# Block products for the third group of the down projection in layer 0's second feed-forward block

## Chip, cores, metric

One core of a Trainium2 chip runs the whole kernel in one launch. The metric is the device time of that launch in microseconds (us), the median of several runs. Engines are named as in the profile: PE (TensorE, matmuls), PEld (its weight loads), DVE (VectorE), ACT (ScalarE), POOL (GpSimd), SP (SyncE, here a queue that only issues transfers).

## The reference, cut to what matters

Two layers over 528 tokens (512 and 16 meta tokens) of width 1024. Each layer is feed-forward, mixer, feed-forward; the last layer is followed by a norm. All in float32.

```
def swiglu(x, w_gate, w_up, w_down):            # D_FF = 2816
    return (jax.nn.silu(x @ w_gate) * (x @ w_up)) @ w_down

for l in range(DEPTH):                          # DEPTH = 2
    h = h + 0.5 * swiglu(rmsnorm(h, norm_gains[l, 0]), ffn_w_gate[l, 0], ffn_w_up[l, 0], ffn_w_down[l, 0])
    h = h + mixer(rmsnorm(h, norm_gains[l, 1]), ...)
    h = h + 0.5 * swiglu(rmsnorm(h, norm_gains[l, 2]), ffn_w_gate[l, 1], ffn_w_up[l, 1], ffn_w_down[l, 1])
return rmsnorm(h, final_norm)[:, N_META:]
```

The case concerns `ffn_w_down[0, 1]`, the down projection of the second feed-forward block of layer 0, which the kernel calls block (0, 1).

## The kernel before, in words

**Layout.** h is held transposed on the chip, as 8 tiles of 128 channels by 528 tokens (`hall`, `h(m)`). Every float32 operand of a matmul is split into a rounded part and a residual: `whi` (L310, ACT) and `wlo` (L311, DVE) for weights, `hi` and `lo` for the moving operand. A product takes three matmuls for each pair of tiles: hi by hi, hi by lo, lo by hi. Half of the tokens, 264, go into one matmul.

**Block products.** Gate and up projections use Strassen's method in Winograd's form: a 2 x 2 split of both matrices, seven block products (numbered 1 to 7) in place of eight. For the weights the blocks 11, 12 and 22 are loaded as they are (`DIRECT`), the four others are sums, made by accumulating transfers on POOL's queue (L224), by ACT negations (L219, L277), and in part by DVE. For the moving operand, `Norm.pair(j)` makes from two tiles of h seven parts, each split into hi and lo (lines 526 to 552: ACT L532, L539, L544, DVE L540, L545, L547, L548, L550, L551).

**Groups.** The 22 hidden tiles come as 11 pairs, in groups of 4, 4 and 3 pairs (`GROUPS`). After the pairs of a group, the group's share of the down projection is added to h. It can go two ways:

- direct: `down(g, m, first, last)` runs `product` (L488) for each output tile m over the group's hidden tiles. In the third group, two of the tiles have begun between the products of the group's last pair, tiles 0 to 3 are held until the last two hidden tiles are there, tiles 4 to 7 follow one by one. When tile m is complete, `add_to_h` adds it (L587), `lower_h` scales h(m) by the norm factor (L592), and `done(m)` starts the next block's operand.
- by block products: `operands_of`, `operand` and `difference` (L700, L701, L703, L706, L710) make the moving operands from the hidden tiles, and `fast_down(g, dq, c, part)` (matmuls L745) runs product c for quad dq (four tiles of h each). Each result is added at once to two tiles of h by DVE (L753). In the third group the last eleven products come in the order `CLOSING`, and `PACE = 0` has all eight `lower_h` and `done` stand behind the last of them in program order.

**Which way.** `fast_groups(f)` gives the number of groups that go by block products: all three for the blocks in `ALL_FAST`, two for the others. With `f = (l, f)`:

```
GROUPS = (4, 4, 3)
ALL_FAST = [(0, 0), (1, 0)]
CLOSING = tuple(zip((1, 0, 1, 0, 0, 0, 1, 1, 1, 1, 1), "16273456734"))
def fast_groups(f):
    return len(GROUPS) - (f not in ALL_FAST)
```

`ffn_steps` lists the steps of a block: P is a gate/up product, D a direct piece of the down projection, O the making of operands, S a block product of the down projection. `weight_plan` turns them into the order in which weights are loaded. A direct third group takes its weights from `wts` in 6 slabs of 512 KB; a block-product group loads 5 blocks a quad from `win` (384 KB each in the third group) and adds 4 accumulating transfers a quad.

**What comes after a block.** Blocks (0, 0) and (1, 0) are followed by the mixer; their `done` is `b.chunk`, one plain operand a tile (L516, L517) and its square. Block (0, 1) is followed by block (1, 0); its `done` is `d.pair_of`, which runs `Norm.pair` once both tiles of a pair are there. Block (1, 0) begins with products 1 and 2 of pairs 0 and 1, then 6 and 5 of pair 0; at the latter the squares of h are summed (L526) and the mean of the norm is a matmul against a constant (L494).

**Order.** The program is written in one order and a planner, run when the kernel is built, moves instructions ahead on each engine by readiness and program order; on the chip each engine then runs its own list in order. Weights are made up to three products ahead (`AHEAD_MADE`) into four buffers each for `whi` and `wlo`, and fetched up to nine loads ahead into three buffers.

Of the kernel before, what the change touches and what calls it, by code (L numbers as in the profile page):

```python
# [39 lines left out]


GROUPS = (4, 4, 3)
ALL_FAST = [(0, 0), (1, 0)]
LAST = [sum(GROUPS[: g + 1]) - 1 for g in range(len(GROUPS))]
QUADS = 2
LATE = 5
# [9 lines left out]
def fast_groups(f):  # L56
    return len(GROUPS) - (f not in ALL_FAST)

# [1375 lines left out]
```

## Time and profile before

| | |
|---|---|
| time, median of 3 runs | 2187.26 us (2186.92 to 2187.61) |
| span of the profiled execution | 2185.6 us |
| the profiled execution's own time | not given apart; the median is 1.7 us above the span |
| PE busy | 2149.1 us, 98% |
| DVE busy | 1802.6 us, 82% |
| ACT busy | 1245.9 us, 57% |
| third group of block (0, 1), direct | 1026.9 to 1111.7 us |
| third group of block (0, 0), block products | 279.6 to 362.5 us |
| third group of block (1, 0), block products | 1374.2 to 1456.9 us |

The span runs from the first to the last instruction. Busy time is the union of an engine's instructions; a matmul's record overlaps the next one's, so the pace of matmuls is read from their starts. Row forms: a timeline row gives start, length, engine, line, operation, output and inputs, shape, count and, in brackets, the idle time before it and what ended it; a group row gives count, busy time and mean; a wait row gives total, times and longest.

### The profile page before, as it was taken

How to read it: one execution, taken by the hardware profiler on the slowest of the kernel's cores; microseconds unless marked ns; L12 is line 12 of the kernel's file. 1: busy time of each engine (PE TensorE's matmuls, PEld its weight loads, DVE VectorE, ACT ScalarE, POOL GpSimd, SP SyncE). 2: the span in 40 equal slices, each digit the busy share in tenths (PEclk: the TensorE clock that was granted, in tenths of full speed). 3: DMA queues.
4: the chain of work that ended last, by engine and by line, in shares of the span. 5: the costliest groups of instructions: out<-in, count | busy, mean ns of one | idle time of the engine just before them, and what ended most of it. 6: DMA issues, size and time to landing. Idle time of an engine off the chain costs nothing.

```text
span 2185.6 us, 40161 instructions
## 1 busy us (share of the span) xinstructions
PE 2149.1 (98%) x16434; PEld 2056.1 (94%) x16434; DVE 1802.6 (82%) x2751; ACT 1245.9 (57%) x1844; POOL 119.0 (5%) x140
## 2 busy tenths in 40 slices
PE   7999999999999999999999999999999999999998
PEld 7999999989999999999999999988788888999997
DVE  8887979776976689888789979797779767997986
ACT  8545556444784556454575455574557836554544
POOL 1100000000000000010010000000000001000100
PEclk9999999999999999999999999999999999999999
DMA  9866755212113467676567667553121146775751
GB/s 286 218 195 182 202 154 139 82 51 76 49 40 123 130 177 180 202 185 183 167 162 187 199 181 204 153 140 97 49 78 49 49 135 152 199 204 178 196 162 68
DMA packets 91223, 320.32 MB, mean 147 GB/s; under 512 B 10144, under 2 KB 12576, under 8 KB 91040
## 3 DMA queue, kind: packets, MB, share of 16 engines
q1 hardware_dynamic: 70048, 246.58, 33.9%
q0 software_dynamic: 19584, 69.21, 17.6%
q8 instruction: 129, 2.11, 0.4%
q10 hardware_dynamic: 1408, 1.97, 0.3%
q14 instruction: 54, 0.44, 0.1%
HBM read 294.65 MB, written 2.10 MB: 136 GB/s over the span
## 4 chain that ended last, share of the span: by engine, by line
PE 83%; DVE 9%; ACT 4%; DMA 2%; issue 2%; SPq 0%; DVEq 0%; ACTq 0%
PE ss L621 36%; PE mm L488 15%; PE ss L745 14%; PE ss L488 7%; DVE wlo L311 3%; PE sm L488 2%; DMA w<-win 2%; PE sm L1125 1%; PE ss L1100 1%; ACT whi L310 1%; PE ss L494 1%; DVE h L753 1%; PE sm L1141 1%; PE ss L1101 1%; PE sm L1142 1%
## 5 line engine op out<-in xcount | busy, mean ns | idle before, releaser
L621 PE MATMUL ss<-xc,whi 128*128 128x264 f32 (+1 forms) x4928 | 903.1, 285 | 11.3 <-ACT whi L310 7.4
L621 PEld LDWEIGHTS ss<-xc,whi 128*128 128x128 f32 x4928 | 764.5, 189 | 14.9 <-ACT whi L310 8.0
L621 PE MATMUL ss<-xc,wlo 128*128 128x264 f32 (+1 forms) x2464 | 700.6, 285 | 4.0 <-DVE wlo L311 4.0
L311 DVE TENSOR_TENSOR wlo<-w,whi 128x1024 fp32r<-128x1024 f32 (+2 forms) x355 | 423.7, 1200 | 66.7 <-ACT whi L310 66.3
L621 PEld LDWEIGHTS ss<-xc,wlo 128*128 128x128 f32 x2464 | 465.0, 189 | 5.9 <-DVE wlo L311 5.9
L310 ACT CAST whi<-w 128x1024 fp32r<-128x1024 f32 (+2 forms) x355 | 362.1, 1036 | 169.3 <-PE ss L621 80.1
L488 PE MATMUL mm<-x,whi 128*128 128x264 f32 (+1 forms) x1712 | 385.5, 315 | 0.0
L488 PEld LDWEIGHTS mm<-x,whi 128*128 128x128 f32 x1712 | 278.1, 188 | 16.3 <-issue 1.0
L745 PE MATMUL ss<-g,whi 128*128 128x264 f32 (+1 forms) x1520 | 284.3, 285 | 3.6 <-DVE h L753 1.7
L488 PE MATMUL mm<-x,wlo 128*128 128x264 f32 (+1 forms) x856 | 266.3, 316 | 0.0
L745 PEld LDWEIGHTS ss<-g,whi 128*128 128x128 f32 x1520 | 236.2, 188 | 7.5 <-DVE g L706 3.6
L745 PE MATMUL ss<-g,wlo 128*128 128x264 f32 (+1 forms) x760 | 215.2, 283 | 0.0
L625 ACT COPY c<-ss 128x528 f32<-128x528 f32 (+1 forms) x132 | 78.4, 594 | 239.0 <-PE ss L621 238.7
L310 ACT CAST whi<-raw 128x1024 fp32r<-128x1024 f32 x114 | 119.3, 1048 | 130.7 <-PE mm L488 94.2
L311 DVE TENSOR_TENSOR wlo<-raw,whi 128x1024 fp32r<-128x1024 f32 x114 | 139.0, 1220 | 57.2 <-ACT whi L310 53.2
L488 PEld LDWEIGHTS mm<-x,wlo 128*128 128x128 f32 x856 | 159.6, 188 | 8.5 <-issue 0.5
L745 PEld LDWEIGHTS ss<-g,wlo 128*128 128x128 f32 x760 | 143.0, 188 | 0.0
L224 POOL DMA_DIRECT2D w<-win x64 | 56.1, 876 | 1453.2 <-DVE t L1261 342.0
L745 PE MATMUL ss<-c,whi 128*128 128x264 f32 (+1 forms) x608 | 115.5, 285 | 0.3
L311 DVE TENSOR_TENSOR wlo<-s,whi 128x1024 fp32r<-128x1024 f32 (+1 forms) x94 | 112.2, 1195 | 1.6 <-ACT whi L310 1.4
L467 ACT ACTIVATE c<-c 128x528 f32<-128x528 f32 (+1 forms) x88 | 56.5, 642 | 98.5 <-DVE c L671 98.4
L488 PE MATMUL ss<-g,whi 128*128 128x264 f32 (+2 forms) x516 | 103.6, 310 | 0.0
(270 smaller groups left out, 3379.1 us busy)
## 6 DMA issues: line engine op xcount, KB each, us to landing
w<-win SPq DMA_DIRECT2D x333, 512.0 KB, 4.4
raw<-wts SPq DMA_DIRECT2D x114, 512.0 KB, 3.3
w<-win POOLq DMA_DIRECT2D x60, 512.0 KB, 7.5
s<-win POOLq DMA_DIRECT2D x26, 512.0 KB, 7.5
w<-s POOLq DMA_DIRECT2D x26, 512.0 KB, 6.1
w<-win SPq DMA_DIRECT2D x20, 384.0 KB, 3.6
s<-w POOLq DMA_DIRECT2D x8, 512.0 KB, 7.4
h<-xt SPq DMA_DIRECT2D x3, 528.0 KB, 6.0
```

Source lines behind the costliest of these rows:

```text
L224: self.nc.gpsimd.dma_start(t, src, accum_op=ALU.add)
L310: nc.scalar.copy(hi[:, cs], w[:, cs])
L311: nc.vector.tensor_tensor(lo[:, cs], w[:, cs], hi[:, cs].bitcast(F32), ALU.subtract)
L467: prev_act[0] = S.activation(*args, **kw).ins
L488: TE.matmul(acc.half[i][:width], lhs, rhs[:, acc.spans[i]], start=first, stop=last)
L494: TE.matmul(a, weights, x[:, hs], start=True, stop=True)
L621: TE.matmul(acc[:, j], a[:, j, k], b[:, at], start=bool(begin and k == 0 and i == 0), stop=k == len(x) - 1 and i == 2, skip_group_check=no ...
L625: W.behind = S.copy(part(st, q), acc).ins
L745: closing[0] = TE.matmul(acc[:, j], a[:, j, k], xs[b][:, k], start=bool(begin and k == 0 and i == 0), stop=k == n - 1 and i == 2, skip_gro ...
L753: V.tensor_tensor(to, to, acc, ALU.add)
L1100: TE.matmul(s[:n, i, :HF], lhs, kh[:, hs], start=True, stop=False)
L1101: TE.matmul(s[:n, i, :HF], lhs, kl[:, hs], start=False, stop=True)
```

## The change

Block (0, 1) is added to `ALL_FAST`, so that its third group also goes by the seven block products, in the steps that blocks (0, 0) and (1, 0) already take. Nothing else in the source changes; `ffn_steps`, `weight_plan` and the layout of the weights in memory follow from it.

```
 GROUPS = (4, 4, 3)
-ALL_FAST = [(0, 0), (1, 0)]
+ALL_FAST = [(0, 0), (0, 1), (1, 0)]
 LAST = [sum(GROUPS[: g + 1]) - 1 for g in range(len(GROUPS))]
```

## The prediction, on record before the result

> **What bounds the kernel now.** I read the page first (span, busy times), then the stage windows, then the waits of TensorE, then the groups of VectorE instructions in two windows.
>
> ```profile
> span 2185.6 us, 40161 instructions
> PE 2149.1 (98%) x16434; PEld 2056.1 (94%) x16434; DVE 1802.6 (82%) x2751; ACT 1245.9 (57%) x1844; POOL 119.0 (5%) x140
> ```
>
> TensorE is busy 98% of the span, so a matmul removed counts in full only if VectorE (82%) keeps pace. The question is whether it does so at this place. Three windows show the third group of three feed-forward blocks, from the start of its last unbroken run of gate/up products to the first matmul of what follows. The first is the block that changes; the other two already close with block products (layer 0 first block, layer 1 first block). Columns: length, then busy time and count of PE, PEld, DVE, ACT, POOL, granted clock, DMA share, GB/s.
>
> ```profile
> 1026.93:1111.67 84.74, 84.74 (x697) 84.74 (x696) 67.25 (x97) 48.15 (x66) 6.12 (x7) 1.00 0.60 161
> 279.55:362.62 83.07, 81.75 (x663) 80.77 (x662) 72.33 (x99) 49.77 (x67) 7.88 (x9) 1.00 0.56 149
> 1374.21:1456.93 82.72, 81.45 (x661) 80.64 (x660) 72.31 (x99) 49.61 (x67) 7.87 (x9) 1.00 0.56 150
> ...
> 1430.00:1457.75 27.75, 26.48 (x207) 25.55 (x207) 27.48 (x38) 18.50 (x25) 1.76 (x2) 1.00 0.58 151
> ```
>
> In the block to be changed TensorE never rests (84.74 of 84.74). In its twins it rests 1.3 us, and in the last 27.75 us VectorE is busy 27.48: it is full there, not TensorE. The waits of TensorE in the twin's stage are two, both on VectorE:
>
> ```profile
> PE ss L745 <- DVE h L753: 0.8, 2, 0.6
> PE ss L745 <- DVE g L706: 0.4, 1, 0.4
> ```
>
> **The change, part by part.** The direct product is 8 output tiles x 6 slices x 3 terms x 2 halves = 288 matmuls. The block products are 2 quads x 7 products x 3 slices x 2 x 3 terms = 252. So 36 go, which is also 697 less 661. At 84.74/697 = 0.122 us each that is 4.4 us at most.
>
> Term 1, the stage. The edited block should look like its twin in layer 1: same shapes, same steps, same blocks ahead of it. Whole stage against whole stage: 82.72 - 84.74 = **-2.0 us** (the layer 0 twin gives 83.07, that is -1.7). Of the 4.4 us, 1.3 go to the two waits and the rest to the slightly longer pace of the block products.
>
> What this term holds without a price of its own: the seven operands' subtractions and residuals (L706, L710, L701), 14 additions to h (L753) for 8 (L587), 14 weight casts and residuals of 768 columns for 6 of 1024, six fewer hidden-tile splits. They are all in the twin's VectorE 72.3 us against 67.3. ScalarE goes from 48.2 to 49.6 us and has room; its work lies beside TensorE's.
>
> Transfers: 6 loads of 512 KB leave the SP queue and 10 of 384 KB come; 8 accumulating transfers come to POOL's queue. I cost them at nothing: in the twin's stage the DMA share is 0.56 against 0.60, and no TensorE wait there is on a transfer. The next block's first loads and sums move behind them on SP and POOL. What could hurt is the buffer of the next first weight block, free only after the last group's negated block is taken:
>
> ```profile
> 1436.95 0.84 ACT L277 ACTIVATE s<-w 128x768 f32<-128x768 f32 x1 [0.40 <-DVE wlo L311]
> 1087.47 0.88 POOL L224 DMA_DIRECT2D s<-win  x1 [25.26 <-ACT s L219]
> ```
>
> In the twin that is 1456.93 - 1436.95 = 20 us before the stage ends; before, the next block's first accumulation starts 24 us before. The summed blocks are wanted only after four products (4 x 24 x 0.122 = 11.7 us) more, so some 30 us remain for a few transfers. If that cover is gone, TensorE waits at the fifth product.
>
> Term 2, the hand-over. This is where the block differs from its twins: they are followed by the mixer, this one by the next feed-forward block, whose operands are built in pairs of seven block sums, not in plain chunks. Before, the direct product finishes h tile by tile, 4.4 us apart, and VectorE lowers h (L592) and builds pairs 0 to 3 meanwhile. With the block products, the first quad's tiles are final only after the sixth of eleven closing turns and the rest with the last two, and the code emits all eight L592 and the four pairs behind the last turn; the planner moves forward only what fits between the additions to h. So work that lay beside matmuls comes at the end. Its price is the work VectorE still owes when the matmuls end. First what it did before from 1090 to the matmul of the norm's mean (L494), the point where TensorE waits for it:
>
> ```profile
> 1090.00:1132.76 42.76, 41.51 (x337) 41.04 (x337) 40.60 (x70) 31.07 (x50) 5.25 (x6) 1.00 0.63 151
> L540 DVE TENSOR_TENSOR xc<-t,xc 128x264 fp32r<-128x264 f32 (+1 forms) x16 | 8.8, 561 | 0.6 <-ACT xc L539 0.5
> L311 DVE TENSOR_TENSOR wlo<-w,whi 128x1024 fp32r<-128x1024 f32 x7 | 8.5, 1216 | 0.8 <-ACT whi L310 0.8
> L592 DVE SCALAR_TENSOR_TENSOR h<-h,rs 128x528 f32<-128x528 f32 x8 | 5.6, 700 | 0.1
> L587 DVE TENSOR_TENSOR h<-h,ss 128x528 f32<-128x528 f32 x8 | 5.5, 693 | 0.0
> L526 DVE TENSOR_TENSOR t<-t,t 128x528 f32<-128x528 f32 x7 | 4.9, 704 | 0.4
> L550 DVE TENSOR_TENSOR t<-t,t 128x264 f32<-128x264 f32 x4 | 1.7, 424 | 0.0
> ...
> L551 DVE TENSOR_TENSOR t<-t,t 128x264 f32<-128x264 f32 x4 | 1.7, 422 | 0.0
> L631 DVE TENSOR_TENSOR c<-c,ss 128x528 f32<-128x528 f32 x2 | 1.4, 694 | 0.0
> L311 DVE TENSOR_TENSOR wlo<-raw,whi 128x1024 fp32r<-128x1024 f32 x1 | 1.2, 1224 | 1.0 <-ACT whi L310 1.0
> L311 DVE TENSOR_TENSOR wlo<-s,whi 128x1024 fp32r<-128x1024 f32 x1 | 1.2, 1217 | 0.0
> ```
>
> (L550, L548, L547, L545, L551 are five such groups of 1.7.) The groups add up to 45.6 us, the engine is busy 40.6: neighbours overlap, so a sum of rows counts 0.89. It is full to 40.6/42.76 = 95%. Now how much of the following block's share the twin had done when its last addition to h ended, at 1457.75:
>
> ```profile
> L753 DVE TENSOR_TENSOR h<-h,ss 128x528 f32<-128x528 f32 x14 | 9.5, 698 | 0.3 <-PE ss L745 0.2
> L311 DVE TENSOR_TENSOR wlo<-raw,whi 128x1024 fp32r<-128x1024 f32 x2 | 2.4, 1220 | 0.0
> L592 DVE SCALAR_TENSOR_TENSOR h<-h,rs 128x528 f32<-128x528 f32 x3 | 2.0, 699 | 0.0
> L517 DVE SCALAR_TENSOR_TENSOR x<-h,par,x 128x528 fp32r<-128x528 f32 x2 | 1.5, 760 | 0.0
> ```
>
> Two weight residuals, and 2.0 + 1.5 = 3.5 us of lowering and operands. The full engine leaves no more. So still owed up to L494: L592 5.6, pairs 8.8 + 5 x 1.7 = 17.3, squares L526 4.9, L631 1.4, six of the eight residuals of the next block 6 x 1.22 = 7.3; together 36.5, less 3.5 = 33.0; times 0.89 = 29.4 us if VectorE never rests, 30.9 us if it rests as before. TensorE's side before:
>
> ```profile
> 1111.67 0.41 PE L621 MATMUL ss<-xc,whi 128*128 128x264 f32 x2
> 1132.76 1.13 PE L494 MATMUL ss<-t,const 128*128 128x264 f32 x4 [1.05 <-DVE t L526]
> 1135.85 0.51 PE L621 MATMUL ss<-xc,whi 128*128 128x264 f32 x2 [0.74 <-ACT c L625]
> ```
>
> From the next block's first matmul to L494: 21.1 us. After: 1457.75 - 1456.93 = 0.8, plus 29.4 to 30.9, so 30.2 to 31.7; the hand-over grows by 9.1 to 10.6 us. If two of the six residuals (for the products behind L494) come after the squares, 2 x 1.22 x 0.89 = 2.2 less, 6.9. The likely order lies between; I take **+9.0 us**. TensorE's cover is gone in pieces: of a new pair's share TensorE has 4 products x 6 x 0.122 = 2.9 us to do, VectorE (17.3 + 5.6)/4 x 0.89 = 5.1 us.
>
> Sum: -2.0 + 9.0 = **+7.0 us** on the execution's span of 2185.6, that is 2192.6. The median of the runs, 2187.26, is 1.7 us above the span; I keep that and forecast 2194.3.
>
> **One rule weighed.** TensorE ran slower at the start of the execution, though the granted clock reads 1.00 there:
>
> ```profile
> 15.06 0.64 PE L621 MATMUL ss<-xc,whi 128*128 128x264 f32 x2
> ...
> 15.72 0.64 PE L621 MATMUL ss<-xc,whi 128*128 128x264 f32 x2
> 19.14 0.41 PE L621 MATMUL ss<-xc,whi 128*128 128x264 f32 x2
> 0.00:10.00 10.00, 2.02 (x6) 1.44 (x6) 5.12 (x13) 7.32 (x13) 1.08 (x5) 1.00 0.83 293
> 10.00:20.00 10.00, 7.94 (x33) 6.54 (x32) 9.12 (x21) 9.35 (x17) 1.69 (x3) 1.00 1.04 346
> 1133.85 0.41 PE L621 MATMUL ss<-xc,whi 128*128 128x264 f32 x2
> ```
>
> The same pair of matmuls took 0.64 us at 15.7 and 0.41 at 19.1. Short waits later did not bring that back (0.41 again 1.1 us after the 1.05 us wait at L494). The Trainium skill, "TensorE: Matmul & The Clock Gate", section "Why this matters for your kernels", says that no idle gaps above about 3 us should stand between bursts, since an idle window brings the half clock back. By that rule the sum would be rival 3's, since the new waits are bursts of 2.9 us in every 5.1 us, or of 1.5 us where only two products have their weights.
>
> **The rivals.**
> 1. Not slower: VectorE reaches the pairs during the closing turns, and the hand-over costs nothing. Then only term 1 is left: 2187.26 - 2.0 = 2185.3. It decides from the point where VectorE does 9 us more of the next block's work before the last block product ends. For it: the first quad's tiles are final some 10 us before the end. Against: the 27.48 of 27.75 us above.
> 2. The hand-over is set by the pairs alone, not by the squares behind them: TensorE gets more products ahead of L494 and the waits of 1.05 + 0.74 us vanish. Pairs are done 0.8 + (5.6 + 17.3 - 3.5) x 0.89 = 18.1 us after the last block product; TensorE has 11.7 us of products, if it can run them as operands come: 6.4 us lost. -2.0 + 6.4 - 1.8 = +2.6, 2189.9. For it: operands are awaited part by part, as the start shows below (TensorE begins at 7.36 with a pair whose last part is written at 9.34). Against: TensorE's order is fixed, and before it stood still at L494 with other products in hand.
> 3. The slow rate returns at the hand-over: up to the 39 matmuls of the start's two windows at 0.22 us (from 15.06 to 15.72 three matmuls in 0.66 us) for 0.122, about +4 on top: 2198.3. Against: the single gaps would be 2 to 3.5 us, at the edge.
>
> ```profile
> 7.36 0.81 PE L621 MATMUL ss<-xc,whi 128*128 128x264 f32 x2 [7.36 <-ACT whi L310]
> 9.34 0.71 DVE L540 TENSOR_TENSOR xc<-t,xc 128x528 fp32r<-128x528 f32 x1
> ```
>
> **How the numbers follow.** Forecast 0.56 (2194.3), rival 2 0.22, rival 3 0.14, rival 1 0.08. The range leaves out rival 1 and the upper part of rival 3: 2188 to 2198.5; the forecast's own, from 6.9 to 10.6 us of hand-over, is 2192.2 to 2195.9. A change within 0.2% (4.4 us) is about what a measurement of this kernel cannot tell from none: rival 2 and most of rival 1 fall there, the forecast and rival 3 are slower. Faster needs the whole 4.4 us and no wait: 0.04.
>
> **What would show it.** Right: 36 matmuls fewer; third group of 82.7 us; then TensorE waits on L540, L592 or L311 between about 1108 and 1135, VectorE above 95% there, L494 some 30 us after the last L745 of that group. Wrong: L592 and pairs already in the closing turns, or waits on transfers of the next block's weights, or matmul pairs of 0.64 us.

## The result, and the profile after

The changed kernel takes 2204.52 us (median of 5 runs, 2203.55 to 2207.06) against 2187.26 us for the kernel before (2186.36 to 2188.10): the ratio is 1.0078, with a 95% interval of 1.0066 to 1.0090. It is 17.3 us slower, where the prediction said 7.0 us slower with a range up to 2198.5. The page of the changed kernel shows that the matmuls went and the time did not:

```profile
span 2201.5 us, 40177 instructions
PE 2151.9 (98%) x16398; PEld 2056.2 (93%) x16398; DVE 1819.3 (83%) x2779; ACT 1256.8 (57%) x1861; POOL 125.9 (6%) x148
```

TensorE has 16398 matmuls for 16434, the 36 fewer that were counted, and yet it is busy 2.8 us longer (2151.9 for 2149.1). Fewer matmuls in more busy time means that some ran slower. The windows say where. The first row is the third group up to the first matmul of the next block, the second goes from there to L494, the others are stretches inside (columns as in the windows above: behind the five engines come the granted clock, the DMA share and GB/s):

```profile
1027.09:1120.48 93.39, 84.63 (x661) 83.17 (x660) 75.62 (x108) 52.97 (x71) 11.24 (x13) 0.96 0.64 163
1120.48:1148.35 27.87, 23.22 (x156) 21.36 (x157) 26.80 (x47) 21.92 (x37) 3.60 (x5) 0.88 0.70 161
1105.90:1112.20 6.30, 0.02 (x2) 0.01 (x1) 1.02 (x3) 0.89 (x2) 0.86 (x1) 0.92 1.08 211
1112.20:1117.94 5.74, 5.74 (x25) 5.51 (x25) 4.72 (x6) 3.63 (x5) 0.00 (x0) 0.50 0.82 249
1128.50:1134.70 6.20, 4.26 (x16) 3.36 (x15) 6.20 (x14) 4.37 (x10) 0.00 (x0) 0.50 0.50 98
```

The stage starts at 1027.09, 0.2 us from where it started before, so nothing ahead of it matters. It is 93.39 us long instead of 84.74: **+8.65 us**, where -2.0 was forecast. The hand-over up to L494 is 27.87 us instead of 21.09: **+6.8**. From L494 to the restart of the products 4.71 us go by instead of 3.09: **+1.6**. That is 17.05 us, of 17.3 between the medians (the two profiled spans lie 15.9 apart; the rest is made up later in the run). Inside the stage, 6.30 us hold no matmul to speak of (0.02 us busy), and the 5.74 us behind them are full of matmuls at a granted clock of 0.50.

The waits of TensorE over this stretch, and the rows at which the stages end:

```profile
PE ss L745 <- ACT whi L310: 6.3, 1, 6.3
PE ss L621 <- ACT xc L539: 3.1, 2, 1.7
PE ss L621 <- ACT c L625: 2.1, 1, 2.1
PE ss L745 <- DVE h L753: 1.1, 2, 0.9
PE ss L621 <- DVE h L753: 0.9, 1, 0.9
...
PE ss L494 <- DVE t L526: 0.5, 1, 0.5
```

```profile
1112.20 1.32 PE L745 MATMUL ss<-g,whi 128*128 128x264 f32 x3 [6.28 <-ACT whi L310]
1120.48 0.48 PE L621 MATMUL ss<-xc,whi 128*128 128x264 f32 x2 [0.89 <-DVE h L753]
1126.26 0.70 PE L621 MATMUL ss<-xc,whi 128*128 128x264 f32 x2 [1.42 <-ACT xc L539]
1130.61 0.90 PE L621 MATMUL ss<-xc,whi 128*128 128x264 f32 x2 [1.65 <-ACT xc L539]
1148.35 1.13 PE L494 MATMUL ss<-t,const 128*128 128x264 f32 x4 [0.51 <-DVE t L526]
1153.06 0.51 PE L621 MATMUL ss<-xc,whi 128*128 128x264 f32 x2 [2.11 <-ACT c L625]
```

The largest wait by far, 6.28 us, is one that the twin does not have: a block product of the closing stage waits for its weights' rounded part. The chain of work names what stood behind that:

```profile
1097.01 3.16 DMA w<-win
...
1100.87 0.62 POOL w L224
1101.48 9.75 DMA s<-w
...
1111.31 0.84 ACT whi L310
```

The wanted weights are the sum for product 3 of the group's second quad: ScalarE negates a block (L277), an accumulating transfer on POOL's queue adds another (L224), ScalarE rounds the result (L310). Here are ScalarE's and POOL's own rows (ScalarE first, then POOL), and then POOL's one row at the same point of the twin in the kernel before:

```profile
1097.84 1.06 ACT L219 ACTIVATE s<-w 128x1024 f32<-128x1024 f32 x1 [1.11 <-DMA w<-win]
1098.81 0.83 ACT L277 ACTIVATE s<-w 128x768 f32<-128x768 f32 x1
...
1111.31 0.83 ACT L310 CAST whi<-s 128x768 fp32r<-128x768 f32 x1 [5.61 <-DMA s<-w]
1099.31 0.86 POOL L224 DMA_DIRECT2D s<-win  x1 [14.41 <-DVE h L753]
1100.84 0.86 POOL L224 DMA_DIRECT2D w<-win  x1 [0.67 <-DVE h L592]
1101.48 1.12 POOL L224 DMA_DIRECT2D s<-w  x1
```

```profile
1438.20 0.88 POOL L224 DMA_DIRECT2D s<-w  x1 [5.79 <-ACT s L277]
```

The negation L219, on 1024 columns, belongs to the next block, (1, 0). Its sums are begun when its weights are *fetched*, nine loads ahead, so in program order it comes before the group's own negation L277, and ScalarE takes its list in order. In the twin L277 ran at 1436.95, which is 62.7 us into the stage, ahead of three weight casts; here the three casts come first, then ScalarE stands 1.11 us for the next block's load, and only behind L219 comes L277, at 1098.81, 71.7 us into the stage, 9 us later. So the standing is 1.1 us of the 9; the rest is the place in the list. POOL then issues the next block's two accumulations of 512 KB (1099.31, 1100.84) ahead of the group's own (1101.48). That one lands after 9.75 us; the twin's took 4.9 (the DMA view's median of its single issue), with nothing else on POOL's queue. Together the sum lands 15.2 us later in the stage than in the twin: 9.0 by L277, 1.4 more until POOL issues it, 4.8 in the transfer. Whether the transfer is slow for what stands ahead of it in POOL's queue or for the load of the DMA engines (share 1.08 in the stop) is not separated here. VectorE has a hole at the same place (5.28 us of idle ahead of its next residual), so the stop is not even used for the work that it owes.

### The profile page after: what moved, and what is told of

It is laid out like the page before. It is cut to its first block, busy times and chain, and to the rows that moved or that the text cites. A ratio compares the mean times of both kernels' runs of the same rounds, so it can differ in the third digit from the quotient of the medians.

```text
span 2201.5 us, 40177 instructions
## 1 busy us (share of the span) xinstructions
PE 2151.9 (98%) x16398; PEld 2056.2 (93%) x16398; DVE 1819.3 (83%) x2779; ACT 1256.8 (57%) x1861; POOL 125.9 (6%) x148
## 3 DMA queue, kind: packets, MB, share of 16 engines
q1 hardware_dynamic: 70624, 247.36, 33.3%
q8 instruction: 129, 2.11, 0.4%
## 4 chain that ended last, share of the span: by engine, by line
PE 83%; DVE 9%; ACT 4%; DMA 2%; issue 2%; SPq 0%; DVEq 0%; POOL 0%; ACTq 0%; POOLq 0%
PE ss L621 36%; PE mm L488 15%; PE ss L745 15%; PE ss L488 6%; PE sm L488 2%; DVE wlo L311 2%; DMA w<-win 1%; PE sm L1125 1%; ACT whi L310 1%; DVE h L753 1%; PE ss L1100 1%; DVE g L706 1%; PE ss L494 1%; PE sm L1141 1%; PE ss L1101 1%
## 5 line engine op out<-in xcount | busy, mean ns | idle before, releaser
L621 PE MATMUL ss<-xc,whi 128*128 128x264 f32 (+1 forms) x4928 | 906.3, 285 | 17.5 <-ACT whi L310 7.4
L621 PEld LDWEIGHTS ss<-xc,whi 128*128 128x128 f32 x4928 | 766.3, 189 | 22.4 <-ACT whi L310 7.8
L621 PE MATMUL ss<-xc,wlo 128*128 128x264 f32 (+1 forms) x2464 | 701.2, 285 | 3.6 <-DVE wlo L311 3.6
L311 DVE TENSOR_TENSOR wlo<-w,whi 128x1024 fp32r<-128x1024 f32 (+2 forms) x365 | 433.8, 1196 | 67.5 <-ACT whi L310 66.9
L310 ACT CAST whi<-w 128x1024 fp32r<-128x1024 f32 (+2 forms) x365 | 370.0, 1031 | 177.4 <-PE ss L621 86.0
L621 PEld LDWEIGHTS ss<-xc,wlo 128*128 128x128 f32 x2464 | 466.0, 189 | 5.4 <-DVE wlo L311 5.4
L745 PE MATMUL ss<-g,whi 128*128 128x264 f32 (+1 forms) x1640 | 309.6, 286 | 11.7 <-ACT whi L310 6.3
L745 PEld LDWEIGHTS ss<-g,whi 128*128 128x128 f32 x1640 | 256.7, 190 | 16.8 <-ACT whi L310 8.3
L745 PE MATMUL ss<-g,wlo 128*128 128x264 f32 (+1 forms) x820 | 233.0, 285 | 0.0
L625 ACT COPY c<-ss 128x528 f32<-128x528 f32 (+1 forms) x132 | 78.5, 595 | 243.7 <-PE ss L621 243.5
L310 ACT CAST whi<-raw 128x1024 fp32r<-128x1024 f32 x108 | 113.0, 1048 | 123.6 <-PE mm L488 93.7
L311 DVE TENSOR_TENSOR wlo<-raw,whi 128x1024 fp32r<-128x1024 f32 x108 | 131.8, 1222 | 54.0 <-ACT whi L310 50.1
L745 PEld LDWEIGHTS ss<-g,wlo 128*128 128x128 f32 x820 | 155.3, 190 | 0.0
L224 POOL DMA_DIRECT2D w<-win x66 | 57.9, 877 | 1426.4 <-DVE wlo L311 606.9
L745 PE MATMUL ss<-c,whi 128*128 128x264 f32 (+1 forms) x656 | 124.6, 285 | 0.4
L753 DVE TENSOR_TENSOR h<-h,ss 128x528 f32<-128x528 f32 (+1 forms) x154 | 106.1, 698 | 8.6 <-PE ss L745 7.9
```

The costliest lines, as they stand in the source:

```text
L224: self.nc.gpsimd.dma_start(t, src, accum_op=ALU.add)
L310: nc.scalar.copy(hi[:, cs], w[:, cs])
L311: nc.vector.tensor_tensor(lo[:, cs], w[:, cs], hi[:, cs].bitcast(F32), ALU.subtract)
L621: TE.matmul(acc[:, j], a[:, j, k], b[:, at], start=bool(begin and k == 0 and i == 0), stop=k == len(x) - 1 and i == 2, skip_group_check=no ...
L625: W.behind = S.copy(part(st, q), acc).ins
L745: closing[0] = TE.matmul(acc[:, j], a[:, j, k], xs[b][:, k], start=bool(begin and k == 0 and i == 0), stop=k == n - 1 and i == 2, skip_gro ...
```

## Experiments

Each ratio is against the kernel before on the same chip: its medians there were 2189.10 us for the first four kernels, 2188.39 for the next four and 2187.63 for the last three. The start of the stage lies anywhere from 1025.9 to 1029.6 us in the profiles, so stages are compared by their lengths.

**1. The group's last weight sum made by VectorE (s4_on_vector).** The changed kernel with the sum for product 3 taken off ScalarE and POOL:

```
-            if i < NPAIR + QUADS * (len(GROUPS) - 1):
+            if i < NPAIR + QUADS * (len(GROUPS) - 1) or f == (0, 1):
                 V.tensor_tensor(s4, w, self.kept, ALU.subtract)
```

> The changed kernel with one sum made elsewhere: for the third group of block (0, 1) the weight sum of block product 3 is one VectorE subtraction of 768 columns (0.95 us) a quad, in place of a ScalarE negation and an accumulating transfer on POOL's queue. Theory 1 (the group's own last weight sum comes late, because the next block's negation and two 512 KB accumulations stand ahead of it on ScalarE and POOL): the stop of 6.3 us in the closing turns goes, and with it the half-clock stretch of 5.7 us behind it (2.9 us lost): -8 to -10 against the changed kernel, 2194 to 2197. Rival (VectorE is full and sets the end whatever the transfers do): the two subtractions add 1.8 us to VectorE and the wait returns on VectorE: 2203 to 2206.

Measured: 2200.91 us, ratio 1.0057 (1.0045 to 1.0070). The stop of 6.28 us is gone, and no wait in the closing products is over 0.54 us, but the time that theory 1 named, 2194 to 2197, is missed: another wait comes at the first products of the next block:

```profile
1114.04 2.00 ACT L219 ACTIVATE s<-w 128x1024 f32<-128x1024 f32 x2 [3.85 <-DMA w<-win]
...
1116.57 0.71 ACT L539 CAST xc<-t 128x264 fp32r<-128x264 f32 x2
1117.02 0.90 PE L621 MATMUL ss<-xc,whi 128*128 128x264 f32 x2 [4.39 <-ACT xc L539]
```

The same kind of negation, L219, again stands at the head of ScalarE's list waiting for its load, 3.85 us, and now what is queued behind it are the casts of the next block's operands. TensorE stops 4.39 us for them, and 20.0 us at a granted clock of 0.50 follow (1117.02 to 1136.98). So the group's own sum was the victim; what blocks is the next block's negation.

**2. The next block's sums later (next_sums_later).** The changed kernel, but the first two pairs of block (1, 0) are not fetched before that last weight sum has been made:

```
+            if not isinstance(load, int) and load[0] == (1, 0) and load[1] < 2 and \
+                    self.made <= self.at[(0, 1), NPAIR + 2 * QUADS + 1, "6"]:
+                return
```

> The changed kernel, with the loads and sums of the next block's pairs 0 and 1 written in the program only after the group's last weight sum (two products later). Nothing is computed elsewhere. Theory 1: order alone is the cause; same gain as with the sum on VectorE, -8 to -11 against the changed kernel, 2193 to 2197. Rival (the accumulating transfer is slow because the transfers of the stage crowd each other, whatever their order): the sum still lands late, -3 at most, above 2201.

Measured: 2198.84 us, ratio 1.0045 (1.0033 to 1.0058), the lowest of the complete kernels that hold the change. The three added lines shift its later line numbers by 3 (L624 is L621). The windows are the stage and the hand-over to L494:

```profile
1029.56:1114.96 85.40, 81.61 (x661) 80.62 (x660) 73.33 (x103) 51.43 (x69) 11.36 (x13) 1.00 0.67 175
1114.96:1146.12 31.16, 25.87 (x159) 23.92 (x159) 29.09 (x52) 23.73 (x40) 3.49 (x4) 0.78 0.67 154
```

The stage is 85.40 us, its clock 1.00, and no wait on ACT is left in it. L277 is back at 62.7 us into the stage, and its transfer takes 3.9 us. The hand-over is 31.16 us, inside the 30.2 to 31.7 of the prediction, with VectorE busy 29.09 of them, though it holds 13.7 us at a granted clock of 0.50, which the forecast had not. So 8 of the 8.65 us of the stage came from the next block's sums. From L494 to the restart it takes 3.08 us, as before the change. Not all of the gain stays: work that VectorE did beside and around the stop now falls into the hand-over, 31.16 for 27.87, so that of 17.05 us 0.66 + 10.07 are left; the medians differ by 9.7. The 2193 to 2197 us of theory 1 were missed for that reason.

**3. The order of the hand-over alone (handover_alone).** The kernel before, direct product and all, but with the eight `lower_h` and `done` of block (0, 1) behind the last tile, as the block products have them:

```
-            if g == len(GROUPS) - 1:
+            if g == len(GROUPS) - 1 and (l, f) == (0, 1):
+                for c in range(KC) if m == KC - 1 else ():
+                    lower_h(c, rs)
+                    done(c)
+            elif g == len(GROUPS) - 1:
```

> The kernel before (direct third group), with one edit: in block (0, 1) all eight lowerings of h and the next block's operands are written behind the last tile, as the block products have them. Theory (hand-over: VectorE's work is left to the end by program order): +5 to +9 against before, 2192 to 2196, with TensorE waiting on the pairs' parts. Rival (the planner moves them ahead by readiness, since the direct tiles finish 4.4 us apart): within 1.5 us of before, 2186 to 2189.

Measured: 2189.18 us, ratio 1.0003 (0.9994 to 1.0012). From the next block's first matmul to L494:

```profile
1113.20:1132.81 19.61, 19.09 (x157) 18.91 (x156) 19.05 (x30) 16.38 (x26) 1.77 (x2) 1.00 0.36 93
```

It is 19.61 us, shorter than the 21.09 of before; up to the restart behind L494 it is 24.3 us for 24.2. The program order costs nothing: the planner takes the lowering and the pairs forward again, because in a direct third group VectorE has room (67.25 of 84.74 us busy). What hurts in the changed kernel is that it has none.

**4. One lowering a turn, on top of number 2 (later_and_paced).** 

```
-                for _ in range(len(ready) if (dq, c) == CLOSING[-1] else min(len(ready), PACE)):
+                for _ in range(len(ready) if (dq, c) == CLOSING[-1] else min(len(ready), PACE + ((l, f) == (0, 1)))):
```

> The later next sums, and in block (0, 1) one lowering of h (with its pair) written after each closing turn from the fifth on, in place of all eight behind the last. Theory (program order of the hand-over costs): 2 to 4 us less than the later next sums alone, about 2190 to 2193. Rival (VectorE is full in the closing turns, so work moved ahead there delays the additions to h that TensorE waits for): within 1 us of the later next sums alone, or slower.

Measured: 2200.78 us, ratio 1.0057 (1.0044 to 1.0071), not better than number 2 (the intervals overlap). VectorE takes lowerings and pairs earlier, but the closing products then stop for it: 2.03 us for an addition to h and 1.86 us for a weight residual. Against number 2 the stage grows from 85.40 to 91.94 us, while the hand-over to L494 shrinks from 31.16 to 23.84. Moving VectorE's work between two stretches that it fills moves the wait with it.

**5. The next block's sums begun when cast (negate_when_cast).** The way in which the first block of layer 0 already begins its sums, for block (1, 0): negations and accumulations come when the pair's own weights are made, three products ahead, not at the fetch.

```
-OPENING = ((0, 0), 0), ((0, 0), 1)
+OPENING = ((0, 0), 0), ((0, 0), 1), ((1, 0), 0), ((1, 0), 1)
```

> The changed kernel, with pairs 0 and 1 of block (1, 0) added to OPENING: the ScalarE negations that begin their weight sums, and the accumulations behind them, are written when the block is cast and no longer when its load is issued. Theory 2 (the negations L219 stand at the head of ScalarE's in-order queue and wait for late loads, and the group's last sum, the operands' parts and POOL's transfers stand behind them): both the 6.3 us stop in the closing turns and stops of 2 to 4 us on the operands' parts go; what stays is VectorE's owed work. -9 to -13 against the changed kernel, 1.002 to 1.004 of before (2191 to 2196). Rival (VectorE is full and TensorE's pauses bring the half clock back in any case): not below 1.0045, the later next sums' ratio.

Measured: 2199.78 us, ratio 1.0055 (1.0042 to 1.0067). Stage, hand-over to L494, and a stretch within that:

```profile
1028.60:1112.71 84.11, 81.57 (x660) 80.59 (x660) 73.52 (x104) 50.69 (x68) 10.48 (x12) 1.00 0.67 179
1112.71:1143.57 30.86, 23.69 (x156) 21.38 (x157) 28.78 (x51) 24.41 (x41) 4.38 (x5) 0.89 0.65 157
1122.30:1129.40 7.10, 5.28 (x19) 4.18 (x18) 7.10 (x17) 5.04 (x11) 0.87 (x1) 0.52 0.53 104
```

The largest wait inside the closing products is 0.45 us. The stage is 84.11 us: -0.6 against the direct product. It would be at the twin's 82.7, but the next block's first product comes 1.6 us late (on its weights' cast). The hand-over is 30.86 us, +9.8, with VectorE busy 28.78; L494 still waits 0.8 us for L526, and the restart is again 1.6 us later than before. Together -0.6 + 9.8 + 1.6 = +10.8 us; the medians differ by 11.4. This is the change without its unforeseen part, and it is still 0.55% slower: theory 2's 2191 to 2196 us did not come, and the rival's bound, not below 1.0045, held. The third row is the half clock again, so neither half of the rival, the full VectorE and the clock, is ruled out here.

**6. Both cures together (negate_when_cast_s4_vector).** Numbers 5 and 1 in one kernel.

> The same, with the third group's sum for block product 3 on VectorE as well. If ScalarE's and POOL's order was all of it, nothing is left to gain and the 1.8 us of VectorE cost something: 0 to +2 against the negations at the cast alone. If POOL's transfers still come late there, -2 to -5.

Measured: 2201.94 us, ratio 1.0063 (1.0051 to 1.0076), no better than either. One more subtraction of 768 columns lies on VectorE, the next block's first product waits 3.35 us, and the hand-over is 31.4 us (1113.94 to 1145.30).

**7. The lowering given to GpSimd (lower_on_gpsimd).** Number 5, with the norm factor scaled by -0.25 once, and the eight lowerings of block (0, 1) done by GpSimd, which is nearly idle:

```
+                if (l, f, dq, c) == (0, 1, 0, "1"):
+                    V.tensor_scalar(rs, rs, -0.25, None, ALU.mult)
...
-                    lower_h(m, rs)
+                    if (l, f) == (0, 1):
+                        G.tensor_tensor(h(m), h(m), rs, ALU.mult)
+                    else:
+                        lower_h(m, rs)
```

> The negations at the cast, with the eight lowerings of h in block (0, 1) on GpSimd (a multiplication by the norm factor, scaled once by VectorE) in place of VectorE. VectorE sheds 8 x 0.62 less one instruction, 4.3 us. Theory (VectorE's owed work sets the hand-over): -2 to -4 against the negations at the cast alone. Rival (the lowering is a link in the chain h, lowering, operand, and GpSimd is slower at it): 0 to +6.

Measured: 2205.37 us, ratio 1.0078 (1.0064 to 1.0091); 5.2 us are taken from VectorE (8 x 0.70 less one instruction of 0.43) and the kernel is slower, by as much as the rival allowed but not for its reason. VectorE's row at that place, GpSimd's, and TensorE's largest wait:

```profile
1115.60 0.42 DVE L548 TENSOR_TENSOR t<-t,t 128x264 f32<-128x264 f32 x1
1116.06 8.40 DVE L551 TENSOR_TENSOR t<-t,t 128x264 f32<-128x264 f32 x1
1116.32 7.84 POOL L762 TENSOR_TENSOR h<-h,rs 128x528 f32<-128x528 f32 x6
PE ss L621 <- ACT xc L539: 9.9, 2, 8.7
```

A subtraction of 264 columns takes 0.42 us, and the next of the same size 8.40, as long as GpSimd's six multiplications last beside it. The Trainium skill, "SBUF — State Buffer", section "Who interferes with whom", says that a VectorE instruction with two inputs in SBUF and a GpSimd instruction that reads SBUF shut each other out of a shared port. The trace agrees, and it shows that the loser stood through six instructions in a row; beside an earlier multiplication (1108.53) a weight residual of 1024 columns took 2.34 us for 1.21. The engine that is idle on the page was not free for this.

**8. The same edit in the kernel before (before_negate_when_cast).**

> The kernel before (direct third group) with the same edit of OPENING: does the later negation help or hurt by itself? Theory 2: before, the loads landed early enough, so it is worth nothing there, 1.000 plus or minus 0.001. If the sums for products 6 and 5 of pair 0 then come too late, it costs 1 to 4 us.

Measured: 2187.80 us, ratio 0.9999 (0.9990 to 1.0008), with no half clock in that stretch. So when the next block's sums begin makes no difference with a direct third group, whose weights need no sums. It is the pairing of the two that costs.

**9 to 11. What sets the hand-over.** All three are number 5 with an edit. In negate_no_squares the additions L526 are left out for the one norm; in negate_kept_warm matmuls against zeros fill the waits of the first two products; the last has both.

```
-            else:
+            elif self.gc != G_NORM + 3 * KC:
                 V.tensor_tensor(self.acc, self.acc, sq, ALU.add)
...
+                if (l, f, p) == (1, 0, 0) and product in "12" and k in (1, 2):
+                    for i in range(3 * k):
+                        TE.matmul(acc[:, i % 2], zero, xh[:, at], start=False, stop=False, skip_group_check=True)
```

> As negate_when_cast, with the seven additions L526 that sum the squares of h for the norm of block (1, 0) left out (the norm then counts one tile of eight). That takes 7 x 0.70 = 4.9 us from VectorE, 4.4 us at the 0.89 used before. Theory A, VectorE alone sets the hand-over: L494 comes about 4 us sooner after the first product of the next block (26.5 to 27.5 us for 30.86) and the time falls from 2199.8 to about 2196. Theory B, VectorE and TensorE at half clock end together: TensorE's products take the same time, L494 no longer waits 0.83 us for L526, and the time falls by 1 us at most, to about 2199.

> As negate_when_cast, with 3 and 6 matmuls against zero weights added behind the second and third slice of the first two products of block (1, 0), where TensorE otherwise waits for operands; they add zeros, 18 x 0.122 = 2.2 us in waits of 0.5 to 2.3 us. Both theories: if they keep the granted clock at 1.00, the 6.8 us at 0.50 and the 3.4 us that they lose are gone. Theory A, VectorE alone sets the hand-over: L494 stays at 30 to 31 us and waits some 3 us more for L526; the time stays within 1 us of 2199.8. Theory B, VectorE and TensorE end together: the same here. A third, the half clock alone makes the hand-over long: L494 3 us sooner, about 2196.5.

> Both edits together (the norm again counts one tile of eight). Theory A, VectorE alone: the same as negate_no_squares, about 2196. Theory B, VectorE and TensorE at half clock end together: only both edits help, L494 3 to 4 us sooner than in negate_when_cast (27 to 28 us for 30.86), about 2196, where each of the two alone stays near 2199. If the added matmuls do not keep the clock, B gives 2199 here too.

Without the squares, the planner puts L494 further ahead in TensorE's list, so the comparable stretch goes from the first matmul of the next block to the restart behind L494's norm:

The time at half clock is worked out from the granted clock in windows of 1 us.

| | time, us | ratio (95%) | first product to restart, us | of it at half clock, us |
|---|---|---|---|---|
| before (profile of before) | 2187.26 | | 24.18 | 0 |
| negate_when_cast | 2199.78 | 1.0055 (1.0042 to 1.0067) | 35.57 | 6.8 |
| negate_no_squares | 2197.17 | 1.0043 (1.0031 to 1.0056) | 33.89 | 10.2 |
| negate_kept_warm | 2200.34 | 1.0056 (1.0042 to 1.0070) | 35.44 | 6.8 |
| negate_warm_no_squares | 2195.25 | 1.0038 (1.0025 to 1.0050) | 33.30 | 3.4 |

The windows of the stretch, one for each kernel in the order of the table's last four rows:

```profile
1112.71:1148.28 35.57, 26.28 (x173) 23.63 (x173) 30.20 (x54) 27.89 (x47) 4.38 (x5) 0.90 0.69 170
```

```profile
1111.06:1144.95 33.89, 27.07 (x172) 24.71 (x173) 27.22 (x49) 27.70 (x47) 4.41 (x5) 0.85 0.69 158
```

```profile
1111.43:1146.87 35.44, 28.62 (x190) 26.31 (x190) 29.72 (x52) 27.89 (x47) 4.38 (x5) 0.90 0.70 170
```

```profile
1110.10:1143.40 33.30, 27.44 (x190) 25.43 (x191) 27.18 (x49) 27.71 (x47) 4.41 (x5) 0.95 0.70 161
```

Taking 4.9 us from VectorE brings the restart 1.7 us nearer. Theory A had asked for some 4 us, theory B for 1 at most; neither number came (the medians differ by 2.6, with intervals that overlap). The half clock grew from 6.8 to 10.2 us at the same time, which may hide a part of VectorE's share. The added matmuls did not shorten the half clock by themselves (6.8 us in both, half of it now behind a wait of 2.4 us ahead of the first product), so negate_kept_warm tells nothing on what the half clock costs. Between the two kernels without squares the half clock shrinks from 10.2 to 3.4 us and the stretch by 0.6; the two medians lie within each other's intervals. That suggests, without showing it, that most of the half clock is covered by waits for operands there. For negate_warm_no_squares both theories had named about 2196, so its 2195.25 does not decide between them. What is shown: VectorE is a part of the bound, and neither it nor the clock alone is the whole. How the rest divides among VectorE, ScalarE (busy 27.7 of 33.3 us) and the weights' loads stays open.

No version here beats the kernel before. The cures of the stop (numbers 1, 2 and 5) recover a third to not quite a half of the 17.3 us that the change costs, by their medians; most of the rest is the hand-over.

## Why the prediction was wrong

**The step that failed: "Transfers: ... I cost them at nothing."** It went by two signs from the twin, a DMA share of 0.56 and no wait on a transfer, and said that the next block's first sums "move behind" the group's. They move ahead of them: they are begun at the fetch, nine loads early, and stand in front on ScalarE and POOL. The row at 1436.95 was in the prediction, as the moment when a buffer comes free; it was not followed to the one instruction that another block's work could now push back. The twin has no such neighbour, as what follows it is the mixer. The price in the changed kernel: 6.28 us of stop and 5.74 us at half clock, which is 2.9 us lost, 9.2 us of the stage's error of 10.65. (Of the 1.5 us left, 1.2 are waits on additions to h, 1.1 + 0.9 where the twin had 0.8.) Numbers 2 and 5 show it by taking it away: the stage comes back to 85.40 and 84.11.

**Term 1, -2.0 us.** Mis-sized by 1.4 even without the stop: 84.11 in number 5, or -0.6. The closing products themselves kept the twin's pace (the last L745 starts 82.24 us into the stage), but the next block's first product waits 1.6 us.

**Term 2, +9.0 us, with L494 at 30.2 to 31.7 us.** Near in size where the stop is removed: 31.16 and 30.86 us, that is +10.1 and +9.8, VectorE 93% busy. The mechanism, work that a full VectorE owes at the end, is right in part only, and that the size fits so well is partly luck: both hand-overs hold half clock (13.7 and 6.8 us) that the sum did not have, and taking 4.9 us of the owed work away brought the restart only 1.7 us nearer. In the changed kernel the hand-over reads 27.87, +6.8, since part of the debt was paid around the stop: VectorE is busy 75.62 us in that stage, 73.33 in number 2's. Four of the eight L592 and the sums of one pair come before the next block's first product there, which the prediction had named as a sign of being wrong. The sum left out the restart: from L494 to the products' restart the changed kernel and number 5 take 1.6 us more than before, with ScalarE's c (L625) awaited for 2.1 us.

**Rival 1, not slower,** is out: a hand-over that costs nothing exists only beside a direct product (handover_alone). **Rival 2, pairs alone,** is out too: its waits were to vanish, and they are 0.51 and 2.11 us.

**Rival 3, the half clock,** happened, with a weight of 0.14, in every kernel that has the change. Its objection, that single gaps would be "at the edge", does not hold: the second stretch in the changed kernel (the window from 1128.50 lies inside it, granted clock 0.50) begins at 1128.2, and the longest gap since the first stretch is 1.42 us (the gap of 1.65 us lies behind the fall, inside the stretch); TensorE was busy 1.75 of the 3.41 us ahead of it. In negate_kept_warm the second fall, at 1125.6, came after gaps of 1.56 and 1.31 us. The rule of the Trainium skill that was weighed ("TensorE: Matmul & The Clock Gate", "Why this matters for your kernels") names gaps above about 3 us; the trace agrees for the 6.28 us stop, where the half clock is granted before the stop ends (0.92 on average over it), and goes beyond it for the short gaps. The price of the half clock was 2.9 us where matmuls filled the stretch; in the hand-over it is not shown, and numbers 9 to 11 suggest little.

So the direction was right. Without the stop the change costs 9.7 us (number 2) to 11.4 us (number 5), where 7.0 was forecast and the range ended at 11.2. Of number 5's 10.8 us in the profile, 3.8 were not in the sum: 1.4 of the stage, 0.8 of the hand-over, 1.6 of the restart. The way from there to 17.3 us, well outside the range, is the one wait that no term held, with the half clock behind it.

## What to carry to other kernels

When a stage is predicted from a twin elsewhere in the same run, compare also what comes behind it: work that the next stage issues ahead enters the same in-order lists, and one instruction that is put ahead there, or waits for its load, holds up everything queued behind. An edit that saves TensorE 4 us and adds work to an engine that is already full there costs more than it saves, and curing the largest wait returns only part of it, as the debt of the full engine comes due later. Ask of every new wait whether it also brings TensorE's clock down, for then it is paid again behind it.

## What the hardware showed unexpectedly

- The granted clock fell to 0.50 in the changed kernel with no gap above 1.42 us since the last stretch, TensorE busy 1.75 of the 3.41 us ahead of the fall (1124.83 to 1128.24), and stretches at half clock lasted from 3.4 us (negate_warm_no_squares) to about 20 us (s4_on_vector).
- Six GpSimd multiplications of 528 columns (1.3 us each) held one VectorE subtraction of 264 columns for 8.40 us instead of 0.42.
